# A scale row made by TensorE in four groups of output partitions

## The chip, the cores and the metric

The kernel runs on one core of a Trainium2 chip. The metric is the device time of one execution in microseconds (us), given as the median of several runs. TensorE appears in the profile as PE (its weight loads as PEld), VectorE as DVE, ScalarE as ACT, GpSimd as POOL, and SyncE, which issues most transfers, as SP.

## The reference

The kernel computes one layer of a diffusion backbone on 512 latent tokens and 256 context tokens of width 1024, all in f32. Cut to what matters here:

```python
mx = split(silu(c)     @ w_ada + b_ada, 9)     # modulation of the latent tokens
mc = split(silu(c_ctx) @ w_ada + b_ada, 9)     # modulation of the context tokens

def ffn_sublayer(h_in, shift, scale, gate, norm_w, w1, w3, w2):
    h = rms_norm(h_in, norm_w) * (1 + scale) + shift
    return h_in + 0.5 * gate * ((silu(h @ w1) * (h @ w3)) @ w2)

x   = ffn_sublayer(x,   mx[0], mx[1], mx[2], norm1_w, ffn1_w1, ffn1_w3, ffn1_w2)
ctx = ffn_sublayer(ctx, mc[0], mc[1], mc[2], norm1_w, ffn1_w1, ffn1_w3, ffn1_w2)
...   # token mixing (attention and a gated MLP), then a second ffn_sublayer on x
```

`w_ada` has 1024 rows and 9 x 1024 columns. The change concerns the products that make the first `scale`, `silu(c) @ w_ada[:, 1024:2048]` and the same for `c_ctx`.

## The kernel before

Tokens lie along the free dimension and features along the 128 partitions, so a tensor of width 1024 is eight blocks (`NK = 8`) of 128 features. Products that need f32 precision split each operand into a high and a low part and take three products (`hh`, `hl` are the parts of the modulated input, `oph`, `opl` those of a weight unit).

The kernel begins with a first loop over the eight feature blocks, written out by hand. For block k it makes the scale and the shift, from these the modulated input of block k, and multiplies it with the weights of the first two feature tiles of the first FFN (`step_mm`, `first_half`, `first_ctx`). So the first products start while most of the input is still on its way. The parts of one step:

- SP loads a *scale* tile (128 x 1024 of `w_ada`, 512 KB), a *shift* tile (512 KB) and a *raw* tile of weights (256 KB) for each block. Scale tiles have three buffers; a tile's buffer comes free when its row is done.
- The scale of 128 features is a *row* of eight products on PE (`ada_row`): the stationary operand is `sc[:, kt, :]`, two columns (silu of `c` and of `c_ctx`), the moving one 128 x 128 of the scale tile; the result, 2 x 128 in `pa`, sums over the eight `kt`.
- ACT copies the row out of PSUM (`ada_copy`, the tile `row`), PE turns it into a column of 128 partitions by a product with a 2 x 2 identity (`ada_col`), and ACT adds the bias and multiplies with the norm's weight: the tile `a`.
- The shift goes another way: DVE multiplies and sums 128 x 1024 (`ada_sum`, the tile `junk`), ACT adds the bias (the tile `s`).
- DVE makes `hfull` from x, `a` and the tokens' rms factor `v` (`first_x`), ACT the high part `hh` (`first_h`), DVE the low part `hl` (`first_l`).

Ahead of the loop, PE runs four warm-up products (L288), spreads silu of `c` and `c_ctx` over all partitions (`spread`, L505) for the shift's sums on DVE, and sums the squares of x (`sums`, L465). The second half of these sums stands between row 0 and its column.

Order: within the first loop the instructions of each engine keep the order in which the code is written (`nc.ordered = True`, and `pin` for PE and for the transfers). Step k opens with the column of block k + 1 and the row of block k + 2, so rows run two blocks ahead:

```python
def step_open(k):
    ada_col(row, k + 1)
    if k + 2 < NK:
        ada_row(k + 2)
```

`row` is the last row that ACT copied. The products that follow (`step_mm(k)`, L599) need `hh`, `hl`, `oph` and `opl` of block k. In step 6 the column of block 7 is followed by context products (`first_ctx(2)`, `first_ctx(3)`, L584), and behind these PE has the products of blocks 6 and 7 and the other context products, up to the end of the loop. The rest of the layer then streams its weights through PE.

Of the kernel before, what the change touches and what calls it, by code (L numbers as in the profile page):

```python
# [9 lines left out]
F32 = mybir.dt.float32  # L10
F32R = mybir.dt.float32r
BF16 = mybir.dt.bfloat16
AF = mybir.ActivationFunctionType
ALU = mybir.AluOpType
AX = mybir.AxisListType
PSUM = bass.MemoryType.PSUM

P = 128
D = 1024
NK = D // P  # L20
# [22 lines left out]
COL_QA, COL_KVA, COL_BS, COL_QN, COL_KN, COL_C = 96, 98, 99, 107, 108, 109  # L43
# [130 lines left out]
def layer_kernel(ctx: ExitStack, tc: tile.TileContext, xT, wfirst, wst, wada, wuq, wkpe, cols, wrope, vnw, rope, out):  # L174
    nc = Core(tc)
# [3 lines left out]
    const = ctx.enter_context(tc.tile_pool(name="const", bufs=1))  # L179
# [20 lines left out]
    def mm():  # L200
        return ps.tile([P, 512], F32, tag="mm", bufs=4, name=f"mm_{nc.next_id()}")
# [5 lines left out]
    col = const.tile([P, NCOLS], F32, name="col")  # L207
    ident = const.tile([P, P], F32, name="ident")
# [2 lines left out]
    b1 = const.tile([P, 72], F32, name="b1")  # L211
    pairs = [[const.tile([P, NK, 2], F32, name=f"{n}{i}") for n in "sag"] for i in range(3)]
    mod_s, mod_a, mod_g = ([[pairs[i][n][:, :, j] for j in range(2)] for i in range(3)] for n in range(3))
    sc = const.tile([P, NK, 2], F32, name="sc")
    accs = const.tile([P, NK, 2], F32, name="accs")
    epsc = const.tile([P, 1], F32, name="epsc")
    epsc2 = const.tile([P, 1], F32, name="epsc2")
# [30 lines left out]
    sctx = ExitStack()  # L248
    with right():
        sp = sctx.enter_context(tc.tile_pool(name="start", bufs=2))  # L250

    pin = tc.keep_in_program_order
    nc.scalar.dma_start(col, cols)
# [4 lines left out]
    sblk, units, raws_ = [], [], []  # L258

    def first_scale(k):  # L260
        ra = sp.tile([P, D], F32, tag="sa", bufs=3, name=f"scale_{k}")
        pin(nc.sync.dma_start(ra, wada[k][:, :D]))
        units.append([ra])

    def first_shift(k):
        if k % 2 == 0:
            pool, tag, bufs = (sp, "sb", 1) if k == 4 else (st.raw_pool, "block", BLOCKS)
            sblk.append(pool.tile([P, 2048], F32, tag=tag, bufs=bufs, name=f"shift_{k}"))
        rs_ = sblk[-1][:, (k % 2) * D : (k % 2) * D + D]
        pin(nc.sync.dma_start(rs_, wada[k][:, D:]))  # L270
        units[k].append(rs_)

    def first_raw(k):
        rw = st.raw()
        pin(nc.sync.dma_start(rw[:, :W1], wfirst[k]))
        raws_.append(rw[:, :W1])

    def first_units(k):
        first_scale(k)
        first_shift(k)  # L280
        first_raw(k)

    for k in range(3):
        first_units(k)
    warm = mm()
    nc.scalar.activation(epsc2, epsc, AF.Silu)
    for i in range(4):
        nc.tensor.matmul(two(warm[:, :256]), ones, ones2, start=True, stop=True)  # L288
    nc.scalar.activation(sc.rearrange("p k w -> p (k w)"), col[:, COL_C : COL_C + 2 * NK], AF.Silu)
    nc.scalar.activation(epsc2, sc[:, 0, 0:1], AF.Abs_reciprocal_sqrt, bias=epsc, scale=0.0)  # L290

    def ada_dot(raw, c, which, to=None):
# [32 lines left out]

    def ada_row(d):
        for kt in range(NK):
            pin(nc.tensor.matmul(pa[0:2, :P], sc[:, kt, :], units[d][0][:, kt * P : kt * P + P], start=kt == 0, stop=kt == NK - 1))  # L328

    def ada_copy(d):  # L330
        row = sp.tile([2, P], F32, tag="row", name=f"row_{d}")
        nc.scalar.copy(row, pa[0:2, :P])
        return row

    def ada_col(row, d):
        o = pcol[:, 2 * d : 2 * d + 2]
        pin(nc.tensor.matmul(o, row, ident[0:2, 0:2], start=True, stop=True))
        nc.scalar.activation(
            pairs[0][1][:, d, :], o, AF.Identity, bias=b1n[:, d : d + 1], scale=col[:, COL_N1 + d : COL_N1 + d + 1])

# [159 lines left out]
    pa, pcol = mm(), mm()  # L500
# [49 lines left out]
    oph(0)  # L550
    steps(0)
    ada_row(0)
    row = ada_copy(0)
    late_sums(1)
    ada_col(row, 0)
    ada_sum(0, 0)
    ada_s(0, 0)
# [3 lines left out]
    opl(0)  # L561
    first_units(3)
    ada_row(1)
    row = ada_copy(1)
    first_l(0, 0, 0)
    oph(1)
# [41 lines left out]
# [5 lines that stand above are left out]
    sqs = []  # L613
    first_half(0)
    ada_col(row, 1)
    first_l(0, 0, 1)
    ada_row(2)
    row = ada_copy(2)
    ada_sum(1, 0)
    ada_s(1, 0)  # L620
# [16 lines left out]
    row = ada_copy(3)  # L637
# [12 lines left out]
    row = ada_copy(4)  # L650
# [21 lines left out]
    row = ada_copy(5)  # L672
# [18 lines left out]
    row = ada_copy(6)  # L691
# [19 lines left out]
    row = ada_copy(7)  # L711
# [426 lines left out]
    for f in range(NFIRST, NPLAIN1):  # L1138
# [7 lines left out]
        for w in range(2):  # L1146
            pair = None
            for g in (1, 0) if last else (0, 1):
# [12 lines left out]
                for k in range(NK):  # L1161
                    c = slice(k % 4 * P, k % 4 * P + P)
# [128 lines left out]
    def in_want(i, w):  # L1291
        if w == 0:
            inw[i].append(st.half(wst, U_IN + i))
        src = inw[i][0][:, w * 512 : w * 512 + 512]
        inw[i].append(homes[2] if i == 2 and w else st.pair())
        hi, lo = inw[i][-1]
        nc.scalar.copy(hi, src)
        return lambda: nc.vector.tensor_sub(lo, src, hi.bitcast(F32))

    TILES = (0, 1, 2, 1, 2, 1, 1, 0)  # L1300
    for dt in range(NK):
        w = in_want(dt - 5, 0) if dt > 4 else None
# [537 lines left out]
    for i in range(3, LAST):  # L1840
# [15 lines left out]
        p = (i - 7) // 2  # L1856
# [377 lines left out]
```

## Time and profile before

| what | value |
|---|---|
| median of 3 runs | 1128.44 us (1128.26 to 1128.64) |
| the profiled execution's own time | 1128.48 us |
| its span, first to last instruction | 1126.7 us |
| PE busy | 1121.9 us (100%) |
| DVE busy | 906.7 us (80%) |
| ACT busy | 539.8 us (48%) |
| POOL busy | 307.2 us (27%) |
| granted TensorE clock, mean | 1.000 |
| the eight rows (L328), PE busy | 15.3 us |

Rows of a timeline read: start in us from the span's start, duration in us, engine, line, operation, the tile written <- the tiles read, the shapes, the count; in brackets the idle time of the engine just before it and what ended that. PE rows show the stationary operand's shape as rows*columns. Rows of groups read: busy time in us, mean ns of one, then the idle time ahead of them. Rows of stages read: the stretch, its length, then for each engine busy time and count, and at the end the granted clock, the DMA engines' share and GB/s. An f32 product is recorded as two instructions on PE.

### The profile page before, as it was taken

To read this page: it belongs to the slowest core of one execution; us is meant where nothing else is said; L and a number is where in the kernel's file an instruction comes from. 1 tells how busy PE (TensorE), PEld (TensorE's weight loads), DVE (VectorE), ACT (ScalarE), POOL (GpSimd) and SP (SyncE) were. 2 spreads that over 40 slices of the span, in tenths; PEclk is the share of its full clock that TensorE was granted. 3 is DMA by queue.
4 is the path that set the end of the run, shared out by engine and by line. 5 is a ranking of instruction groups with operands and counts; after the bars stand their busy time and mean duration, and the time that the engine had idled before them with its cause. 6 is when DMAs were issued, how large, how long until landed. Compare 5 with 4: busy or idle time off the path is not lost.

```text
span 1126.7 us, 18766 instructions
## 1 busy us (share of the span) xinstructions
PE 1121.9 (100%) x7078; PEld 1072.4 (95%) x7078; DVE 906.7 (80%) x1667; ACT 539.8 (48%) x1119; POOL 307.2 (27%) x268
## 2 busy tenths in 40 slices
PE   9999999999999999999999999999999999999998
PEld 7799999999999999999988889999999999898997
DVE  6989999888887788866856999978887869686884
ACT  5555422431344214444745569975544535353451
POOL 0002402311333022300018427740014434161330
PEclk9999999999999999999999999999999999999999
DMA  9630354244333764312243211003131423233302
GB/s 349 213 114 19 116 184 129 98 148 150 102 129 144 243 205 171 128 54 83 85 141 94 65 38 39 20 24 127 57 98 60 146 73 110 83 108 112 113 1 94
DMA packets 35674, 125.89 MB, mean 112 GB/s; under 512 B 3712, under 2 KB 10624, under 8 KB 30976
## 3 DMA queue, kind: packets, MB, share of 16 engines
q1 hardware_dynamic: 35440, 124.63, 32.7%
q8 instruction: 56, 0.92, 0.3%
q14 instruction: 34, 0.28, 0.1%
q10 hardware_dynamic: 144, 0.06, 0.0%
HBM read 122.58 MB, written 2.10 MB: 111 GB/s over the span
## 4 chain that ended last, share of the span: by engine, by line
PE 94%; DVE 4%; ACT 1%; issue 1%; POOL 0%; DVEq 0%; POOLq 0%; ACTq 0%
PE mm L59 57%; PE one L59 20%; PE big L59 8%; PE mm L170 2%; PE mm L168 2%; PE mm L169 2%; PE big L599 1%; PE mm L328 1%; PE mm L584 1%; DVE hfB L59 1%; DVE junk L59 0%; DVE opl L59 0%; PE big L505 0%; PE mm L288 0%; DVE hfull L59 0%
## 5 line engine op out<-in xcount | busy, mean ns | idle before, releaser
L59 DVE TENSOR_TENSOR opl<-block,oph 128x512 fp32r<-128x512 f32 x216 | 192.9, 899 | 32.7 <-ACT oph L59 30.3
L59 POOL TENSOR_TENSOR block<-block 128x512 f32<-128x512 f32 x69 | 104.8, 1518 | 395.3 <-DVE opl L59 392.6
L59 ACT CAST oph<-block 128x512 fp32r<-128x512 f32 x216 | 133.9, 622 | 111.0 <-PE mm L59 84.9
L59 PE MATMUL mm<-gh,oph 128*128 128x384 f32 (+1 forms) x440 | 155.2, 353 | 0.0
L59 PE MATMUL mm<-gl,oph 128*128 128x384 f32 (+1 forms) x440 | 154.9, 352 | 0.0
L59 PE MATMUL mm<-gh,opl 128*128 128x384 f32 (+1 forms) x440 | 154.9, 352 | 0.0
L59 DVE SCALAR_TENSOR_TENSOR x<-mm,g,x 128x256 f32<-128x256 f32 (+2 forms) x184 | 85.0, 499 | 49.4 <-PE mm L59 49.2
L59 ACT CAST oph<-raw 128x512 fp32r<-128x512 f32 x115 | 69.8, 620 | 80.1 <-PE mm L59 59.7
L59 PEld LDWEIGHTS mm<-gh,opl 128*128 128x128 f32 x440 | 82.6, 188 | 5.7
L59 PEld LDWEIGHTS mm<-gh,oph 128*128 128x128 f32 x440 | 82.6, 188 | 5.7
L59 PEld LDWEIGHTS mm<-gl,oph 128*128 128x128 f32 x440 | 82.6, 188 | 5.5
L59 POOL TENSOR_TENSOR block<-s,block 128x512 f32<-128x512 f32 x35 | 46.4, 1325 | 145.0 <-DVE opl L59 144.6
L59 DVE TENSOR_TENSOR opl<-raw,oph 128x512 fp32r<-128x512 f32 x115 | 77.4, 688 | 7.9 <-ACT oph L59 7.2
L59 PE MATMUL mm<-hh,oph 128*128 128x384 f32 x192 | 64.5, 336 | 0.0
L59 PE MATMUL mm<-hl,oph 128*128 128x384 f32 x192 | 64.2, 334 | 0.0
L59 PE MATMUL mm<-hh,opl 128*128 128x384 f32 x192 | 64.1, 334 | 0.0
L59 DVE SCALAR_TENSOR_TENSOR junk<-raw,cb 128x1024 bf16<-128x1024 f32 x48 | 62.2, 1309 | 0.0
L59 POOL TENSOR_TENSOR s<-block 128x512 f32<-128x512 f32 x34 | 53.5, 1572 | 10.7 <-DMA block<-wst 10.7
L59 PE MATMUL one<-hh,oph 128*128 128x384 f32 x144 | 48.1, 334 | 0.0
L59 PE MATMUL one<-hl,oph 128*128 128x384 f32 x144 | 48.1, 334 | 0.0
L59 PE MATMUL one<-hh,opl 128*128 128x384 f32 x144 | 48.1, 334 | 0.0
L59 DVE SCALAR_TENSOR_TENSOR raw<-raw,cb 128x1024 f32<-128x1024 f32 x32 | 41.0, 1289 | 6.8 <-DMA raw<-wada 6.8
(683 smaller groups left out, 3431.0 us busy)
## 6 DMA issues: line engine op xcount, KB each, us to landing
raw<-wst SPq DMA_DIRECT2D x77, 512.0 KB, 3.9
block<-wst SPq DMA_DIRECT2D x36, 1024.0 KB, 4.9
raw<-wada SPq DMA_DIRECT2D x56, 512.0 KB, 4.2
scale<-wada SPq DMA_DIRECT2D x8, 512.0 KB, 7.5
shift<-wada SPq DMA_DIRECT2D x8, 512.0 KB, 8.2
x<-xT SPq DMA_DIRECT2D x5, 512.0 KB, 6.3
raw<-wfirst SPq DMA_DIRECT2D x8, 256.0 KB, 6.8
out<-x SPq DMA_DIRECT2D x7, 256.0 KB, 2.2
```

Source lines behind the costliest of these rows:

```text
L59: return lambda *a, **k: self.tc.keep_in_program_order(f(*a, **k))
L168: nc.tensor.matmul(out, lh, rh, start=first, stop=False, skip_group_check=more)
L169: nc.tensor.matmul(out, lh, rl, start=False, stop=False, skip_group_check=more)
L170: nc.tensor.matmul(out, ll, rh, start=False, stop=last, skip_group_check=more)
L328: pin(nc.tensor.matmul(pa[0:2, :P], sc[:, kt, :], units[d][0][:, kt * P : kt * P + P], start=kt == 0, stop=kt == NK - 1))
L584: pin(nc.tensor.matmul(o, l[:, c], r, start=k == 0 and m == 0 and w == 0, stop=k == NK - 1 and m == 2, skip_group_check=True))
L599: pin(nc.tensor.matmul(two(pbs[i]), l[:, c], lat(r, k), start=False, stop=k == NK - 1 and m == 2, skip_group_check=True))
```

## The change

The eight products of a row go to four groups of 32 output partitions, two products to each group. For this the stationary operand becomes 32 columns wide: a tile `sc` of 128 x 8 x 32, cleared once, whose first two columns of each block hold the two vectors (the other 30 stay zero). Group q holds the sum over kt = q and kt = q + 4. The row is then 128 x 128, and the product that turns it into a column also adds up the four groups: its other operand, `sel`, has a one wherever the partition is 0 (or 1) modulo 32. The tile `sc` moves from the kernel's constants to the pool of the first loop.

```diff
-    sc = const.tile([P, NK, 2], F32, name="sc")
...
+    scw = sp.tile([P, NK, 32], F32, bufs=1, name="sc")
+    sc = scw[:, :, 0:2]
+    sel = sp.tile([P, 2], F32, bufs=1, name="sel")
+    nc.vector.memset(scw, 0.0)
...
+    nc.vector.tensor_reduce(sel, ident.rearrange("p (q c) -> p c q", c=32)[:, 0:2, :], axis=AX.X, op=ALU.add)
     warm = mm()
...
-    nc.scalar.activation(sc.rearrange("p k w -> p (k w)"), col[:, COL_C : COL_C + 2 * NK], AF.Silu)
+    nc.scalar.activation(sc, col[:, COL_C : COL_C + 2 * NK].rearrange("p (k w) -> p k w", w=2), AF.Silu)
...
     def ada_row(d):
         for kt in range(NK):
-            pin(nc.tensor.matmul(pa[0:2, :P], sc[:, kt, :], units[d][0][:, kt * P : kt * P + P], start=kt == 0, stop=kt == NK - 1))
+            q = slice(kt % 4 * 32, kt % 4 * 32 + 32)
+            pin(nc.tensor.matmul(pa[q, :P], scw[:, kt, :], units[d][0][:, kt * P : kt * P + P], start=kt < 4, stop=kt >= NK - 4))
 
     def ada_copy(d):
-        row = sp.tile([2, P], F32, tag="row", name=f"row_{d}")
-        nc.scalar.copy(row, pa[0:2, :P])
+        row = sp.tile([P, P], F32, tag="row", name=f"row_{d}")
+        nc.scalar.copy(row, pa[:, :P])
         return row
 
     def ada_col(row, d):
         o = pcol[:, 2 * d : 2 * d + 2]
-        pin(nc.tensor.matmul(o, row, ident[0:2, 0:2], start=True, stop=True))
+        pin(nc.tensor.matmul(o, row, sel, start=True, stop=True))
```

No instruction changes its place. On PE, around rows 0 and 1, stood before (the row's products are L328 and write 2 x 128; L337 is the column; L465 the second sums of squares; L591 the first weight products):

```order
L328 MATMUL mm_155<-scale_125,sc 2x128 x8
L465 MATMUL mm_165<-sq_4_196,ones 128x256
L465 MATMUL mm_165<-sq_7_203,ones 128x256
L337 MATMUL mm_157<-ident,row_232 128x2
L328 MATMUL mm_155<-scale_132,sc 2x128 x8
L591 MATMUL big_283<-hh,oph_217 128x256 x2
```

and stands now (all lines are five higher):

```order
L333 MATMUL mm_158<-scale_127,sc 32x128 x8
L470 MATMUL mm_168<-sq_4_199,ones 128x256
L470 MATMUL mm_168<-sq_7_206,ones 128x256
L342 MATMUL mm_160<-sel,row_235 128x2
L333 MATMUL mm_158<-scale_134,sc 32x128 x8
L596 MATMUL big_286<-hh,oph_220 128x256 x2
```

The count and the order are the same; the products of a row write 32 partitions each, and the column reads `sel`. On DVE, at the program's start, two instructions are new, the clearing of `sc` and the making of `sel`, both ahead of the first square of x:

```order
L220 MEMSET ones 128x128
L222 MEMSET epsc 128x1
L223 MEMSET nhalf 128x8
L253 MEMSET sc 128x256
L288 TENSOR_REDUCE sel<-ident 128x2
L59 TENSOR_TENSOR sq_0_177<-x 128x512
```

Before, the square stood right behind `nhalf`.

## The prediction

> **What bounds the kernel now.** I read the busy time by stage first, to see which engine has no time left where the change lies.
>
> ```profile
> core 0: us, PE busy (x) PEld busy (x) DVE busy (x) ACT busy (x) POOL busy (x), PEclk, DMA share, GB/s
> 16.00:36.00 20.00, 20.00 (x137) 15.26 (x135) 19.31 (x34) 11.64 (x30) 0.00 (x0) 1.00 1.06 381
> 36.00:52.00 16.00, 16.00 (x98) 12.67 (x96) 14.25 (x28) 7.97 (x21) 0.00 (x0) 1.00 0.38 121
> 66.00:120.00 54.00, 54.00 (x315) 53.94 (x314) 48.35 (x85) 28.97 (x64) 12.03 (x8) 1.00 0.19 59
> ```
>
> Three resources are full at once from 16 to 36 us: PE for 20.00 of 20.00, DVE for 19.31, and the DMA engines at a share of 1.06. Behind 66 us PE has no gap, and DVE has room. So PE time that is saved ahead of 66 us counts only as far as DVE and the transfers let PE use it. The second view is PE's timeline, with the rows that the change touches (L328 a scale row, L337 its column) and the one wait that PE has.
>
> ```profile
> 12.20 1.91 PE L328 MATMUL mm<-scale,sc 128*2 128x128 f32 x16
> 14.04 1.13 PE L465 MATMUL mm<-sq,ones 128*128 128x256 f32 x4
> 15.10 0.38 PE L337 MATMUL mm<-ident,row 2*128 2x2 f32 x2
> ...
> 32.83 0.38 PE L337 MATMUL mm<-ident,row 2*128 2x2 f32 x2
> ...
> 51.78 0.39 PE L584 MATMUL mm<-hh,oph 128*128 128x256 f32 x1
> 52.38 0.38 PE L584 MATMUL mm<-hl,oph 128*128 128x256 f32 x1 [0.21 <-DVE hl L59]
> ```
>
> An f32 product is recorded as two instructions, so x16 is one row of eight products. A row holds PE from 12.20 to the next start at 14.04: 1.84 us. At 52.38 PE waits 0.21 us for DVE's `hl`, and that is the handover which matters: until then PE and DVE run neck and neck, and from there PE works without a break into the following stage. The third view, the chain that ended last, says the same.
>
> ```profile
> 32.90 0.32 PE mm L337 x2
> ...
> 52.38 3.02 PE mm L584 x23
> ```
>
> Between these two rows the chain stands on DVE and ACT alone, over 19 us. So the time at which the first loop ends is DVE's time, and the question is how much DVE waits for a scale row.
>
> **The change part by part: the products of a row.** Rows of the groups between 12 and 52 us, and one weight load of another width from the whole run:
>
> ```profile
> L328 PE MATMUL mm<-scale,sc 128*2 128x128 f32 x128 | 15.3, 272 | 0.0
> L328 PEld LDWEIGHTS mm<-scale,sc 128*2 128x2 f32 x128 | 10.2, 85 | 3.2 <-issue 0.3
> L59 PEld LDWEIGHTS mm<-hh,kpw 128*64 128x64 f32 x16 | 2.1, 134 | 0.0
> L59 ACT COPY row<-mm 2x128 f32<-2x128 f32 x8 | 2.0, 245 | 1.4 <-PE mm L328 1.4
> ```
>
> Eight rows of 16 records cost 15.3 us of PE. No row of the trace shows products in different groups of output partitions, so a new row is bounded from both sides. If the four groups stream at the same time, a quarter of 1.84 us is left, 0.46. If none does, and the loads of 32 columns (between the 85 ns of 2 columns and the 134 of 64) stand in the open by the whole difference, it is 1.84 + 16 x 0.049 = 2.62. I take about 0.8, nearer the lower end: in these rows each load, 85 ns of the 115 that one record takes, already lies beside the stream before it, so the streams are what is left, and they now go to separate output partitions. [...]
>
> **What a shorter row is worth.** PE's saving as such is 8 x (1.84 - 0.8) = 8.3 us. What arrives is what DVE stops waiting. DVE's waits between 15 and 44 us, with the instruction ahead where it is needed:
>
> ```profile
> 15.21 0.08 DVE L59 DVE_READ_ACCUMULATOR junk<-shift,cb 128x1 f32 x1
> 15.90 0.48 DVE L59 SCALAR_TENSOR_TENSOR hfull<-x,a,v 128x256 f32<-128x256 f32 x1 [0.60 <-ACT a L59]
> 28.96 0.75 DVE L59 SCALAR_TENSOR_TENSOR hfull<-x,a,v 128x512 f32<-128x512 f32 x1 [0.18 <-ACT a L59]
> 32.58 0.69 DVE L59 TENSOR_TENSOR opl<-raw,oph 128x512 fp32r<-128x512 f32 x1
> 33.63 0.75 DVE L59 SCALAR_TENSOR_TENSOR hfull<-x,a,v 128x512 f32<-128x512 f32 x1 [0.36 <-ACT a L59]
> 40.70 0.75 DVE L59 SCALAR_TENSOR_TENSOR hl<-hfull,s,hh 128x512 fp32r<-128x512 f32 x1 [0.79 <-ACT hh L59]
> 43.31 0.42 DVE L59 SCALAR_TENSOR_TENSOR v<-mm,r 128x256 f32<-128x256 f32 x1 [0.72 <-ACT r L59]
> ```
>
> Three of them end with `a`, which ACT makes from the column (L337). ACT's rows around them:
>
> ```profile
> 13.57 0.63 ACT L59 CAST oph<-raw 128x512 fp32r<-128x512 f32 x1
> 14.14 0.26 ACT L59 COPY row<-mm 2x128 f32<-2x128 f32 x1
> 15.51 0.35 ACT L59 ACTIVATE a<-mm,b1n,col 128x2 f32<-128x2 f32 x1 [1.12 <-PE mm L337]
> 28.21 0.48 ACT L59 ACTIVATE s<-accs,col 128x1 f32<-128x1 f32 x2 [1.56 <-DVE junk L59]
> 28.59 0.33 ACT L59 ACTIVATE a<-mm,b1n,col 128x2 f32<-128x2 f32 x1
> 32.70 0.29 ACT L59 ACTIVATE s<-accs,col 128x1 f32<-128x1 f32 x1 [0.33 <-DVE junk L59]
> 33.25 0.35 ACT L59 ACTIVATE a<-mm,b1n,col 128x2 f32<-128x2 f32 x1 [0.25 <-PE mm L337]
> ```
>
> - The wait of 0.60. The copy of row 0 stands behind a cast on ACT and starts at 14.14 whatever the row takes; it ends at 14.40. Before the column PE has the second sums (14.04 to 15.10, 1.06 us). With a row of 0.8 they end at 12.20 + 0.8 + 1.06 = 14.06, so the column starts at about 14.5 instead of 15.10. From the column's start to `a` it is 0.41, from there to `hfull` 0.39: `hfull` at 15.30, where DVE is just done (15.21 + 0.08). The whole 0.60 goes. This holds for a row up to 1.24 us; above, the wait comes back one for one.
> - The wait of 0.18 stays: ACT's `a` at 28.59 already stands right behind two `s`, and these wait for DVE itself.
> - The wait of 0.36. `a` came 0.55 after the start of `s`, held by the column; in the row at 28.59 `a` follows its neighbour by 0.38 for two `s`, so 0.19 for one. Then it starts at 32.89 and `hfull` 0.38 later at 33.27, where `opl` ends (32.58 + 0.69). The 0.36 goes, and asks of PE only 0.36 us over five rows.
> - The waits of 0.79 and 0.72 are DVE waiting for ACT for what DVE itself made just before; no PE row is in them. They stay, and are late next, with DVE's work.
>
> DVE's chain moves up by 0.60 + 0.36 = 0.96 us. PE stood ready at 52.17 and must stand ready at 51.42: 0.75 us in eight rows, 0.09 each. Everything behind 52.38 starts 0.96 earlier, with DVE by as much, so the distances in the next stage are unchanged.
>
> **The rest of the change.** The tile `sc` is cleared and `sel` made on DVE ahead of its first square, and ACT's `sc` now waits for the clearing.
>
> ```profile
> 0.82 0.17 DVE L221 MEMSET ones<- 128x128 f32 x1 [0.82 <-PEq L2222]
> 1.00 0.29 POOL masks.py:199 TENSOR_SCALAR_AFFINE_SELECT ident<-ident 128x128 f32<-128x128 f32 x1
> 4.30 0.22 ACT L289 ACTIVATE sc<-col 128x16 f32<-128x16 f32 x1 [1.61 <-DMA col<-cols]
> 5.04 1.29 DVE L59 TENSOR_TENSOR sq<-x 128x512 f32<-128x512 f32 x2 [4.04 <-DMA x<-xT]
> ```
>
> A clearing of twice the width of `ones` is some 0.3 us and the reduction of 64 elements a head less than 0.5; both fit into 4.04 us in which DVE waits for x, and `ident` is there at 1.29. ACT waits for `col` until 4.30, long after the clearing. Cost 0; without that cover 0.8 us. The copy of a row reads 128 partitions instead of 2 with the same 128 elements in each: 245 ns as before. The column now sums 128 rows of weights instead of 2 and still loads 128 columns: 0.31 us from 15.10 to the next row, taken as unchanged; it was 8 x 0.31 = 2.5 us in all, so even a tenth either way is 0.25 us of PE time, of which PE now has some to spare. No DMA is added or moved; scale buffers come free earlier, but the share of 1.06 shows that the engines could not move more by 36 us.
>
> **The sum.** The profiled execution took 1128.48 us (span 1126.7 and 1.8 around it): 1128.48 - 0.96 = 1127.52. The median is 0.04 lower. Forecast: 1127.5 us, 0.09% less. The likeliest case's own range is 1126.5 to 1128.0: to 1128.0 where rows stay between 1.24 and 1.7 us and half of the 0.96 comes; to 1126.5 if the wait of 0.79 or 0.72 shrinks as well, since PE and ACT are then ahead.
>
> **The rivals.**
> - *Nothing streams at the same time.* A row stays at 1.84, the change doesn't do what it says, and DVE's waits stay: 1128.4 us. For it: f32 products, two records each, and no row of this trace with two groups. A start-up cost up to 0.5 would lie here, 1128.9. 11%.
> - *Loads of 32 columns come into the open, slower.* Each product now loads sixteen times the columns into another part of the array than the one that streams; if stream and load then take turns, a row is up to 2.62 us, PE is again the only bound, and PE's chain to 52.38 grows by 8 x 0.78 - 0.21 = 6.0 us: 1134.4. It decides from 2.15 us a row on, where 8 x 0.31 - 0.21 passes 0.2%. [...] Against it: the load beside the stream in the rows of before. 11%.
> - *The clock falls, slower.* PE will now wait some 8.3 - 0.96 = 7 us between 12 and 52 where it had no wait. The first products of the run took 3.78 us for 8 records, twice the 1.91 of the same shape at 7.71 us:
>
> ```profile
> 1.03 3.78 PE L288 MATMUL mm<-ones 128*128 128x256 f32 x8 [1.03 <-DVE epsc L223]
> 7.71 1.91 PE L465 MATMUL mm<-sq,ones 128*128 128x256 f32 x8
> ```
>
>   One such stretch costs 1.9 us, two 3.8: 1127.5 + 3.8 = 1131.3. Against it: the 7 us come in about ten pieces, one before each column or product of the loop. 3%. [...]
> - *DVE is not the bound, much faster.* Then the whole saving arrives, at a row of 0.46 8 x 1.38 = 11.0 us: 1117.4. Against it: DVE's 19.31 of 20 us. 5%, for a part of it.
>
> **How the numbers follow.** Forecast 70%, nothing at the same time 11%, loads 11%, clock 3%, much faster 5%. The range takes the first two with their bounds, 1126.5 to 1128.9, and leaves out 19%. 0.2% is 2.26 us, about what a measurement of this kernel can tell from no change. Faster by more than that: the last rival and a little of the likeliest case's lower end, 0.07. Slower: 0.14. Same: 0.79.
>
> **What the next profile would show.** Right: rows of L328's successor well under 1.2 us; DVE's waits at `hfull` for `a` down to the one of 0.18, those of 0.79 and 0.72 still there; many short PE waits for DVE and ACT between 12 and 52 us; the first wait for `hl` in the context products at about 51.4 and longer than 0.21; the granted clock 1.00. Wrong: rows of 1.8 us or more, PE without a wait there, a lower clock, or DVE waits that are new.

## The result and the profile after

| | before | after |
|---|---|---|
| median of 8 runs | 1128.49 us | 1125.33 us (1124.24 to 1126.17) |
| ratio, 95% interval | | 0.9972 (0.9961 to 0.9983) |
| the profiled execution, its span | 1128.48, 1126.7 us | 1126.13, 1124.3 us |
| granted TensorE clock, mean | 1.000 | 0.998 |

The change saves 3.2 us, more than the 0.96 forecast and outside the range. The eight runs fall into two groups, four at 1124.2 to 1124.7 and four at 1125.9 to 1126.2; the profiled run is of the second. The mean granted clock is 0.997 or 0.998 in all eight, so the clock fell somewhere in each of them; the profile and the experiments below show a fall that costs time, and one that does not.

First the rows and the handover, PE's timeline of the changed kernel (L333 a row, L342 its column, L589 the context products):

```profile
12.23 0.65 PE L333 MATMUL mm<-scale,sc 128*32 128x128 f32 x16
12.80 1.13 PE L470 MATMUL mm<-sq,ones 128*128 128x256 f32 x4
14.45 0.38 PE L342 MATMUL mm<-sel,row 128*128 128x2 f32 x2 [0.52 <-ACT row L59]
14.77 0.42 PE L333 MATMUL mm<-scale,sc 128*32 128x128 f32 x8
...
51.44 0.38 PE L589 MATMUL mm<-hl,oph 128*128 128x256 f32 x1 [0.95 <-DVE hl L59]
```

A row holds PE from 12.23 to 12.80, 0.57 us where it was 1.84. The wait for `hl` now ends at 51.44, 0.94 earlier than at 52.38, and is longer than the 0.21 of before: DVE hands over earlier, and PE stands ready much earlier still. DVE's timeline of the changed kernel has the waits in question:

```profile
15.26 0.49 DVE L59 SCALAR_TENSOR_TENSOR hfull<-x,a,v 128x256 f32<-128x256 f32 x1
28.40 0.75 DVE L59 SCALAR_TENSOR_TENSOR hfull<-x,a,v 128x512 f32<-128x512 f32 x1 [0.18 <-ACT a L59]
32.71 0.75 DVE L59 SCALAR_TENSOR_TENSOR hfull<-x,a,v 128x512 f32<-128x512 f32 x1
39.77 0.75 DVE L59 SCALAR_TENSOR_TENSOR hl<-hfull,s,hh 128x512 fp32r<-128x512 f32 x1 [0.79 <-ACT hh L59]
42.38 0.42 DVE L59 SCALAR_TENSOR_TENSOR v<-mm,r 128x256 f32<-128x256 f32 x1 [0.72 <-ACT r L59]
```

The waits of 0.60 and 0.36 are gone, those of 0.18, 0.79 and 0.72 are there unchanged. Up to here the trace is the one that was forecast. Then come two things that were not. The first stands in the stages of the changed kernel (the number before the last two of a row is the granted clock):

```profile
16.00:36.00 20.00, 16.38 (x142) 12.59 (x146) 19.61 (x35) 11.45 (x32) 0.00 (x0) 1.00 1.06 382
36.00:52.00 16.00, 12.04 (x91) 9.39 (x84) 14.18 (x28) 8.19 (x20) 0.00 (x0) 1.00 0.40 142
52.00:56.00 4.00, 4.00 (x23) 3.90 (x22) 4.00 (x7) 1.52 (x4) 0.00 (x0) 0.58 0.53 185
56.00:60.00 4.00, 4.00 (x19) 3.29 (x18) 4.00 (x9) 1.50 (x4) 0.00 (x0) 1.00 0.43 136
```

PE now waits for 3.6 us in the first stretch and 4.0 in the second, and right behind them the clock falls to 0.58 in the mean of 4 us (0.50 from 52.6 to 55.5). The first product behind the loop is 128x384; its row in before and then in after:

```profile
66.45 0.34 PE L59 MATMUL mm<-hh,oph 128*128 128x384 f32 x1
```

```profile
66.94 0.34 PE L59 MATMUL mm<-hh,oph 128*128 128x384 f32 x1
```

From the first `hl` product to this first product behind the loop it is 66.94 - 51.44 = 15.50 us, and was 66.45 - 52.38 = 14.07. The fall costs 1.43 us, more than the 0.94 gained: at the end of the loop this run is 0.49 us late.

It ends 2.4 us early all the same, so some 2.9 us come from behind the loop, where no instruction was changed. Two products of the timeline that stand 290 products apart, of before and then of after:

```profile
861.06 0.28 PE L59 MATMUL mm<-b11h,oph 128*128 128x256 f32 x1
896.09 0.39 PE L59 MATMUL mm<-gh,opl 128*128 128x512 f32 x1
```

```profile
861.68 0.28 PE L59 MATMUL mm<-b11h,oph 128*128 128x256 f32 x1
896.06 0.39 PE L59 MATMUL mm<-gh,opl 128*128 128x512 f32 x1
```

The same work without a wait takes 35.03 us before and 34.38 after. Grouped by shape in the stretch from 875 to 1000 us, before and after:

```profile
L59 PE MATMUL mm<-t2h,opl 128*128 128x256 f32 x16 | 4.5, 283 | 0.0
L59 PE MATMUL mm<-gh,oph 128*128 128x512 f32 x64 | 24.9, 389 | 0.0
```

```profile
L59 PE MATMUL mm<-t2h,opl 128*128 128x256 f32 x16 | 4.5, 279 | 0.0
L59 PE MATMUL mm<-gh,oph 128*128 128x512 f32 x64 | 24.9, 390 | 0.0
```

The 256-wide products are shorter by 4 ns as recorded (from start to start 120.0 ns before and 117.8 after), the 512-wide ones with `gh` are not.

### The profile page after: what moved, and what is told of

Read it like the earlier page. It is cut to its first block, busy times and chain, and to the rows that moved or that the text cites. A ratio compares the mean times of both kernels' runs of the same rounds, so it can differ in the third digit from the quotient of the medians.

```text
span 1124.3 us, 18769 instructions
## 1 busy us (share of the span) xinstructions
PE 1109.6 (99%) x7078; PEld 1060.7 (94%) x7078; DVE 906.1 (81%) x1669; ACT 540.1 (48%) x1119; POOL 311.4 (28%) x268
## 4 chain that ended last, share of the span: by engine, by line
PE 91%; DVE 6%; ACT 1%; issue 1%; DMA 0%; POOL 0%; SPq 0%; DVEq 0%; POOLq 0%; ACTq 0%
PE mm L59 57%; PE one L59 20%; PE big L59 8%; PE mm L168 2%; PE mm L169 2%; PE mm L170 2%; DVE junk L59 1%; PE mm L589 1%; DVE opl L59 1%; DVE hfB L59 1%; DVE hfull L59 1%; DVE hl L59 1%; PE big L604 1%; DMA x<-xT 0%; DVE v L59 0%
```

## The experiments

What the change does beside its products is to take 64 bytes per partition (`sc`, 8 x 2 x 4) from the constants. The tiles allocated behind it on the left side of SBUF, `oph`, `opl` and `gh` among them, lie 64 bytes lower; those on the right side (`hh`, `hl`, `u`, `t`, most `b`) stay. Theory "place" (L in the expectations): this makes the products faster. Theory "clock" (C): it is the clock's fall, or what comes of it later. The kernels were timed in three sets, each beside the kernel before (median 1128.4 to 1128.5 us in each). In the last set three of its 21 runs lay at 1129.05 to 1129.23 us with a mean clock of 1.000, for a reason that was not looked for; the others lay at 1128.2 to 1128.6.

**Only `sc` moved.** The kernel before, no other edit:

```diff
-    sc = const.tile([P, NK, 2], F32, name="sc")
...
+    sc = sp.tile([P, NK, 2], F32, bufs=1, name="sc")
```

> The kernel before, with only the small tile sc (64 bytes a partition) moved out of the constants into the first loop's pool, as in the change; rows, columns and the order of all instructions stay as before. Every tile allocated behind sc, the weight operands among them, then lies 64 bytes lower, as in the changed kernel. Theory L (place): products of 256 columns run at 117.8 ns instead of 120.0 behind 750 us because of these 64 bytes. Then this kernel has the faster pitch too, and gains about 2.9 us: 1125.6. Theory C (clock): the pitch changes because PE waits and its clock drops in the first loop. Then the pitch stays 120.0 and the time 1128.5.

Measured 1125.37 us, ratio 0.9972 (0.9961 to 0.9982), clock 1.000. Its timeline has the same two products 34.39 us apart:

```profile
860.91 0.28 PE L59 MATMUL mm<-b11h,oph 128*128 128x256 f32 x1
895.30 0.39 PE L59 MATMUL mm<-gh,opl 128*128 128x512 f32 x1
```

So the moved tile alone gives 3.1 us, with every product of the rows as before, and the clock's fall is not what makes the later products faster.

**The change without the new places.** The changed kernel with 64 unused bytes where `sc` was (not shown: one clearing of it at the start, here and in the other kernels with unused bytes):

```diff
+    pad = const.tile([P, NK, 2], F32, name="pad")
```

> The changed kernel with an unused tile of 64 bytes where sc was, so that all later tiles lie at the addresses of the kernel before. Theory L: the pitch of 256 columns is 120.0 again, and only the first loop differs: 0.9 earlier by DVE's waits, 0 to 1.5 us later by the stretch at half clock (52.6 to 55.5 us in the changed kernel): 1127.5 to 1129.0. Theory C: the pitch stays 117.8 and the time 1125.3.

Measured 1127.68 us (1127.51 to 1129.39), ratio 0.9995 (0.9986 to 1.0004). This is the change proper, 0.8 us by the medians; the interval alone does not tell it from nothing. Eight runs lie at 1127.5 to 1127.9 and three at 1129.0 to 1129.4, and the mean clock is 0.997 or 0.998 in all eleven. The profiled one is of the three, with the clock at 0.59 in 52 to 56 us; the 256-wide products from 52.96 to 55.52 us start 0.21 us apart there, and 0.12 ahead of it.

**Rows 5, 6 and 7 in the old way,** the other five as changed, so that PE is busy again from 33 to 48 us (their copies and columns, too, are those of before):

```diff
+    LONE = (5, 6, 7)
...
+            if d in LONE:
+                pin(nc.tensor.matmul(pa[0:2, :P], sc[:, kt, :], w, start=kt == 0, stop=kt == NK - 1))
+                continue
```

> The changed kernel with rows 5, 6 and 7 and their columns made as before (one group of two partitions, 1.84 us a row), so that PE waits some 3.8 us less between 33 and 52 us; rows 0 to 4, on which DVE's two waits hung, stay in four groups, and the addresses are those of the changed kernel. If the waits bring the clock down, the clock stays at 1.00 here, the first loop ends at about 65.5 instead of 66.9, and the two clusters of times of the changed kernel (1124.4 and 1126.1) become one at about 1124.4 or below. If the clock drops for another reason, times as in the changed kernel, 1125.3. Theory C on the pitch would then also have it back at 120.0.

Measured 1124.51 us, ratio 0.9967 (0.9955 to 0.9980); four runs at 1124.5 to 1124.7 and one at 1125.91; the profiled one has the clock at 1.000 throughout. I read this as the cure of the clock. The next kernel shows that it is not: two of these five runs have a mean clock of 0.998, so the clock fell in them, and the profiled run was by chance one of the other three.

**The same at the places of before** (both edits above):

> The changed kernel with the 64 unused bytes per partition that bring every later tile back to its place of before, and with rows and columns 5, 6 and 7 made in the old way, so that TensorE is busy from 36 to 52 us as it was. This leaves the change's two removed waits alone, without the new places and without the fall of the clock. Theory 'two waits' (0.60 and 0.36 us gone, nothing else): every run at 1128.5 - 0.95 = 1127.5 us, none above 1127.9; granted clock 1.000; first wait for hl ends near 51.44, first loop ends near 65.5 us; 256-wide products at 120.0 ns. Rival 'the clock falls all the same': the clock line shows 5 or 6 tenths near 52 to 56 us and some runs are at 1129. Rival 'the gain is given back later': 1128.3 to 1128.5 us with the first loop ending near 65.5.

Measured 1128.79 us (1127.28 to 1129.29), ratio 0.9998 (0.9990 to 1.0007): five runs at 1127.3 to 1127.4, as expected, and six at 1128.8 to 1129.3, which the theory 'two waits' excluded. The stages of the profiled run, one of the six:

```profile
16.00:20.00 4.00, 3.26 (x30) 2.98 (x30) 3.79 (x10) 2.11 (x6) 0.00 (x0) 0.71 1.03 401
48.00:52.00 4.00, 2.51 (x17) 2.10 (x17) 4.00 (x9) 2.53 (x8) 0.00 (x0) 0.98 0.56 174
52.00:56.00 4.00, 4.00 (x23) 4.00 (x23) 3.92 (x8) 1.79 (x5) 0.00 (x0) 0.60 0.62 223
```

PE was busy for all of 36 to 48 us (4.00 of 4.00 in each stage), and the clock fell all the same. What is left ahead of the late fall is 1.5 us of waiting between 48 and 52. This run has an early fall too, at 16 to 20 us.

**Those last waits filled.** In both kernels with old rows 5 to 7, seven products of `ones` into an unread part of a PSUM bank, ahead of the two waits in front of 52 us:

```diff
+                if k == 2 and i == 0 and m < 2:
+                    for _ in range(3 + m):
+                        pin(nc.tensor.matmul(pa[:, 3 * P :], ones, ones, start=True, stop=True, skip_group_check=True))
```

> The kernel with places of before and rows 5 to 7 in the old way, of which 6 runs in 11 lay 1.5 us above the other 5, with seven products of 128x128 by 128 (0.21 us each at their own pitch) that nobody reads put into TensorE's last two waits ahead of 52 us: three ahead of the wait for hh near 49.7, four ahead of the wait for hl near 51. Theory 'those two waits bring the clock down': all runs near 1127.4 us (0.2 either way), none near 1129; the products of 52 to 56 us at the full clock. Rival 'the earlier waits, at 12 to 36 us, do it, or no wait does': both groups of times again, some runs at 1128.8 to 1129.3. If the added products stand in the way themselves, all runs are later by 0.1 to 0.3 us.

Measured 1127.46 us (1127.25 to 1127.56, 11 runs), ratio 0.9990 (0.9981 to 0.9999). Its timeline and stages:

```profile
49.40 0.94 PE L603 MATMUL mm<-ones 128*128 128x128 f32 x6
50.09 0.37 PE L604 MATMUL mm<-hh,oph 128*128 128x256 f32 x1
50.30 1.05 PE L603 MATMUL mm<-ones 128*128 128x128 f32 x8
51.35 0.39 PE L604 MATMUL mm<-hl,oph 128*128 128x256 f32 x1
```

```profile
48.00:52.00 4.00, 4.00 (x32) 3.66 (x31) 3.92 (x10) 2.52 (x8) 0.00 (x0) 1.00 0.66 215
52.00:56.00 4.00, 4.00 (x28) 3.70 (x28) 4.00 (x7) 1.44 (x3) 0.00 (x0) 1.00 0.51 182
```

All eleven runs lie within 0.3 us; the group at 1129 is gone. The added work costs nothing that shows: the first `hl` product starts at 51.35 (51.44 in the changed kernel), and the median is 0.06 us above that of the earlier group of five (1127.40). The clock still falls elsewhere: five of the eleven runs have a mean of 0.998, and they are not slower than the six at 1.000. In the three profiled runs that lie in a later group (the changed kernel, the one with unused bytes, the one with old rows at the places of before) the clock falls behind 52 us; in the profiled run of the earlier group (old rows at the new places) and in both filled kernels it doesn't. So in these runs it is the late fall that costs time, and it goes when the waits in front of 52 us are filled. Without it the two removed waits of DVE are worth 0.93 us. The kernel without the filling was not timed again in this set, which ran on another chip, so a difference between chips is not excluded.

And in the kernel with the places of the changed one:

> The same seven products in the kernel with rows 5 to 7 in the old way and the places of the changed kernel (4 runs in 5 at 1124.5, one at 1125.9). Theory 'the two waits': all runs at 1124.5 us (0.2 either way). Rival: some runs at 1125.9 or 1126.1 still. Either way it is the fastest version so far, and beats the kernel before by about 4 us.

Measured 1124.36 us (1124.18 to 1124.64, 5 runs), ratio 0.9964 (0.9951 to 0.9976): one group, 4.0 us under the kernel before, the fastest version. Its profiled run has a fall in another place, which costs it nothing that shows (1124.43 us, where the two runs with a mean clock of 1.000 took 1124.24 and 1124.36):

```profile
16.00:20.00 4.00, 3.39 (x31) 2.96 (x31) 3.79 (x9) 1.98 (x6) 0.00 (x0) 0.71 1.04 405
52.00:56.00 4.00, 4.00 (x30) 3.72 (x29) 4.00 (x7) 1.66 (x4) 0.00 (x0) 1.00 0.57 205
```

At 16 to 20 us the slower PE only waits less: it is busy for 3.39 us of 4.00 at a clock of 0.71, and for 3.11 at 1.00 in the changed kernel. Behind 52 us, where PE is the bound, a fall was 1.43 us in the changed kernel. Why a run falls early, late, at both places or not at all was not found out; the earlier waits (12 to 36 us) were not filled.

**What is it in the place?** Four layouts of the kernel before, its code otherwise untouched but for the clearing of the unused tile. The left side 64 bytes up:

```diff
+    pad = const.tile([P, NK, 2], F32, name="pad")
```

> The kernel before with an unused tile of 64 bytes ahead of accs, so that all later tiles lie 64 bytes higher instead of lower; nothing else differs but one small clearing. Theory L, if what counts is the place modulo 128 bytes: the same pitch as 64 bytes lower, 1125.6. If the place matters otherwise: another time, from 1125 to 1131. Theory C: 1128.5.

Measured 1125.35 us, ratio 0.9972 (0.9962 to 0.9983).

The left side 128 bytes up:

```diff
+    pad = const.tile([P, NK, 4], F32, name="pad")
```

> The kernel before with 128 unused bytes per partition ahead of the later tiles of the left side: operands move by +128 bytes, twice what +64 did. Theory 'place modulo 128 bytes': as before, 1128.5 us, 256-wide products at 120.0 ns, 512-wide ones at 575 to 650 us at 227 ns. Rival 'any other place than that of before is better': 1125.4 us and 117.8 ns. Rival 'the distance in steps of 64 bytes counts on': something else again, such as 1122 to 1124 us.

Measured 1133.85 us (1133.63 to 1134.27), ratio 1.0049 (1.0036 to 1.0061): slower by 5.4 us, which none of the expectations had. Most of it comes from the 384-wide products, which the changed kernel's layout leaves alone for most of the run (99.86 us for the 576 below). Two that stand 576 apart, in the kernel before and in this one:

```profile
136.16 0.33 PE L59 MATMUL mm<-u2h,oph 128*128 128x384 f32 x1
236.00 0.33 PE L59 MATMUL mm<-u2h,oph 128*128 128x384 f32 x1
```

```profile
137.67 0.34 PE L59 MATMUL mm<-u2h,oph 128*128 128x384 f32 x1
238.41 0.34 PE L59 MATMUL mm<-u2h,oph 128*128 128x384 f32 x1
```

100.74 us instead of 99.84. The 256-wide ones between 875 and 1000 us are 681 as before, but now differ by operands: as recorded 281 ns with `t2h` and `oph`, 285 with `t2h` and `opl`, 284 with `t2l` and `oph`, where before has 283 for all three.

The right side 64 bytes down:

```diff
+    with right():
+        rpad = ctx.enter_context(tc.tile_pool(name="rpad", bufs=1))
+    pad = rpad.tile([P, NK, 2], F32, name="pad")
```

> The kernel before with 64 unused bytes per partition at the top of the right side: hh, hl and the moving operands t1 to t3 and the second stage's scale rows move by -64 bytes, the weights oph, opl and gh stay where they were. Theory 'the distance of the weights from the moving operand counts, modulo 128': 1125.4 us and 117.8 ns for the 256-wide products, as when the weights moved. Rival 'the weights' own place counts': 1128.5 us and 120.0 ns. Rival 'the moving operand's own place counts and it was already the better one': slower than 1128.5 us.

Measured 1125.56 us, ratio 0.9975 (0.9966 to 0.9984), 256-wide products at 281 ns as recorded, where before has 283. The weights didn't move here, only the other operand did.

Both sides 64 bytes down (this edit, and `sc` moved as in the first experiment):

> The kernel before with both sides moved by -64 bytes: the left side as when sc alone was moved (1125.4 us by itself), the right side as with the unused bytes at its top (1125.6 us by itself). Every tile has a new place, but the distance between left and right is that of before. Theory 'the distance counts': 1128.5 us, 256-wide products at 120.0 ns, 512-wide ones at 227 ns. Rival 'each side's own place counts': 1125.4 us or, with both gains, 1122.5 us.

Measured 1128.51 us, ratio 1.0001 (0.9992 to 1.0010), and 35.03 us between the two products again:

```profile
861.08 0.28 PE L59 MATMUL mm<-b11h,oph 128*128 128x256 f32 x1
896.11 0.39 PE L59 MATMUL mm<-gh,opl 128*128 128x512 f32 x1
```

Either side moved alone gives 3 us, both together nothing: what counts is the distance between the weights and the other operand, not the place of either. The traces agree within themselves: the few 256-wide products behind 840 us that have both operands on the left (`gh` or `gl` with `oph`) start 119.1 to 120.0 ns apart both in before and in after. Why the distance counts is not shown. The rule by which a distance is good for a width was not found.

**What makes the rows short.** The changed kernel at the places of before, 32 columns wide, but all eight products into the same 32 partitions; the column reads those 32 alone (not shown: `start` and `stop` as for one sum, the unused 64 bytes, the copy and the column of 32 rows):

```diff
-            q = slice(kt % 4 * 32, kt % 4 * 32 + 32)
+            q = slice(0, 32)
```

> The changed kernel at the places of before, its eight products of a row 32 columns of weights wide as there, but all into the same 32 output partitions and accumulated there one behind the other; only those 32 rows are copied and turned. Theory 'it is the four groups that stream together': a row takes 1.8 us again, DVE's waits of 0.60 and 0.36 us for the scales are back, 1128.5 us (0.3 either way). Rival 'it is the wider weights': rows of 0.6 to 0.8 us and 1127.5 us.

Measured 1128.60 us, ratio 1.0001 (0.9993 to 1.0010). PE's row and two of DVE's waits:

```profile
12.26 1.93 PE L335 MATMUL mm<-scale,sc 128*32 128x128 f32 x16
14.12 1.13 PE L472 MATMUL mm<-sq,ones 128*128 128x256 f32 x4
```

```profile
15.99 0.48 DVE L59 SCALAR_TENSOR_TENSOR hfull<-x,a,v 128x256 f32<-128x256 f32 x1 [0.63 <-ACT a L59]
33.84 0.75 DVE L59 SCALAR_TENSOR_TENSOR hfull<-x,a,v 128x512 f32<-128x512 f32 x1 [0.48 <-ACT a L59]
```

A row takes 1.86 us again (14.12 - 12.26), both waits are back, and the 0.9 us are gone. It is the four groups; the width alone does nothing.

## Why the prediction was wrong

Point by point:

- **A row, 0.8 us from bounds of 0.46 and 2.62.** It is 0.57, nearer the lower end than I took it: within a group of four the records start 7 ns apart where they stood 109 apart. For the sum it makes no difference: any row under 1.24 us is enough.
- **The waits of 0.60 and 0.36 go, those of 0.18, 0.79 and 0.72 stay: 0.96.** Right. `hl` came 0.94 earlier, and with the places held and the late fall filled away (rows 5 to 7 in the old way) the two waits measure 0.93.
- **Edits at the start and the column at nothing.** Right: the clearing of `sc` (0.27 us from 1.00) and `sel` (0.17 from 1.32) end long before the first square of x, the copy of a row takes 251 ns on average against 245, and the column holds PE for 0.32 us (14.45 to 14.77) against 0.31.
- **The rival of nothing streaming together, 1128.4.** Its time is what the row in one group gives, 1128.6, but four groups do stream together. The loads of 32 columns are recorded at 110 ns and don't come into the open: the sixteen of row 0 pass in 0.38 us (12.23 to 12.61). PE isn't the bound: of 8 x (1.84 - 0.57) = 10.2 us that the rows give back, 0.94 arrive.
- **The rival of the clock, at 3%.** It came true: by their mean clocks the clock fell in all eight runs, and by their times it cost something in four. The argument against it, "the 7 us come in about ten pieces", was the mistake: no PE wait of this trace between 12 and 52 us is longer than 1.43 us, and the clock fell. The longest piece alone doesn't decide: the 1.43 us at 34 to 35.5 us had no fall behind it, the 0.87 and 0.95 us in front of 52 had. Nor is a busy share that is enough known: with 3.96 or 4.00 us busy of 4.00 in front of 52 us the clock stayed, with 2.18 (after) or 2.51 it fell, but with 2.47 (the profiled run of the first kernel with old rows 5 to 7) and with 2.22 at 44 to 48 us (after) it stayed. Its price, taken as 1.9 us, measured 1.43 at the late place; the first products of the run, from which it was taken, stand at a recorded clock of 1.00 (0 to 4 us, before), and no run shows what makes them slow.
- **The step that failed: "Everything behind 52.38 starts 0.96 earlier, with DVE by as much, so the distances in the next stage are unchanged".** It took the products behind the loop to last as long as before, since their code is unchanged. The move of `sc` to another pool has no term in the sum, so it stood at nothing without a reason. It shifts every later tile of one side by 64 bytes, and that is worth 3.1 us by itself, three times the change that was meant. The same step left out the late fall of the clock, which adds 1.43 us to the next stage in the profiled run. With the places held, the padded kernel's median of 1127.68 is 0.2 from the forecast. That hangs on most of its runs being in the earlier group: with old rows 5 to 7, where six of eleven are in the later one, the median is 1128.79. What the shift gives lies at the 256-wide products behind 750 us; between 592 and 622 us the 512-wide ones lose 0.51 us by it (30.28 instead of 29.77 between two products 139 apart), and near 823 us PE waits 0.67 us for ACT's `oph`, where it had no wait before, and then 0.23 for `opl` instead of 0.18. Both waits stand in the kernel with only `sc` moved too (0.7 and 0.2).

The sum of the parts, from kernels that isolate them: 0.93 (the two waits) and 3.1 (the distance) are 4.0 us, and the kernel with both and without the late fall measures 1128.39 - 1124.36 = 4.03. The changed kernel itself gets this in half of its runs; the others lose about 1.5 us, which in the profiled one is the late fall.

## What to carry to other kernels

In this kernel, where PE is the bound for most of the run, 64 bytes taken from the constants gave 3.1 us in products whose code was untouched, and 128 bytes put in cost 5.4. When an edit adds, removes or resizes a tile, hold the places with unused bytes before the change itself is judged, and then try a few distances for their own sake. When a stage is made faster ahead of one that PE bounds, look at how busy PE is left in the last microseconds before the handover (here 2.18 us of the 4.00 ahead of the fall): if it is left half idle there, try a handful of products that nobody reads. Here seven of them, in waits that were there anyway, cost nothing that shows, and none of 16 runs was in the later group.

## What the hardware showed that was not expected

- The rate of the products on split operands went with the distance between their two operands in SBUF. In the stage behind 840 us, 256 wide: 120.0 ns from start to start in the layout of before, 117.8 in the changed kernel; as recorded 283 ns before, 279 to 281 with either side moved by 64 bytes, 283 with both. 384 wide, in the layers from 130 to 240 us: 99.84 us for 576 products, 100.74 after 128 bytes, 5.4 us slower in all. Why is not shown.
- In the changed kernel the clock fell for a few microseconds (0.58 in the mean of 52 to 56 us) after waits of at most 1.43 us each. The place differs from run to run, and in the kernels with old rows 5 to 7 some runs have no fall at all (mean clock 1.000 beside 0.997 and 0.998).
- Four groups of 32 output partitions took the f32 row of eight products from 1.84 to 0.57 us, 3.2 times as fast, and 32 columns instead of 2 cost 0.02 us a row in one group (1.86).
